# A two-layer hybrid decoder trunk: the preamble's VectorE and ScalarE work in another order, the keys' norm table and the input's quarter sums moved behind it

## The chip, the cores and the metric

One core of a Trainium2 chip. The time is that of one execution of the kernel on the device, in microseconds (us). The profile is of one such execution, recorded by the hardware profiler; it gives every instruction of the five engines: TensorE (PE in the rows, its weight loads PEld), VectorE (DVE), ScalarE (ACT), GpSimd (POOL) and SyncE (SP), and the DMA transfers.

## The reference

The kernel computes two layers of a decoder trunk for 512 tokens of 2048 features in f32. Each layer is an RMS norm, one wide input projection, three mixers that read slices of it, and an output projection into the residual stream:

```python
h = _rmsnorm(x, norm_g)
proj = h @ w_in                    # 2048 -> conv h,b,c,g  512 each; attention q,k,v,g  1024 each;
                                   #         GLA q,k  256 each; GLA v,g  512 each; GLA low rank  16
y_conv = _short_conv(cv_h, cv_b, cv_c, conv_w, conv_b) * silu(cv_g)
q, k = _rmsnorm(sb_q, sb_qn_g), _rmsnorm(sb_k, sb_kn_g)      # per head of 128
y_sb  = _stick_breaking(q, k, sb_v) * silu(sb_g)
g = log_sigmoid(gl_lr @ gla_w_up + gla_b_up) / 16            # GLA: the decay, from the low-rank part
o = _gla(gl_q, gl_k, gl_v, g)                                # chunked linear attention
y_gla = _rmsnorm(o, gla_on_g) * silu(gl_g)
x = x + concatenate([y_conv, y_sb, y_gla]) @ w_out
```

## The kernel before, in words

The tokens are cut into four tiles of 128 (`NT`), the features into 16 blocks of 128 (`KT`), the columns of each weight matrix into pieces of 256 (`GW`). A list, `specs`, names the pieces in the order of their use: GLA's v in two pieces (the second with the 16 low-rank columns), GLA's q, GLA's k, GLA's gate in two pieces, and then those of the convolution, the attention and the output. Each piece is fetched from memory in f32 into one of two staging buffers (`st`).

A matmul in f32 is done as three matmuls in f16: each operand is split into a high and a low part, and high by high, high by low and low by high are summed in PSUM. For a weight piece this means: a maximum over its squares on ACT (`wmax`, L383), a power of two made of it on DVE (`wscale`, L402 to L417), the high part `wh` on ACT (`whi`, L454; L445 and L447 for the very first piece) and the low part `wl` on DVE (`wlo`, L461).

From the GLA gate on, the pieces in the set `quick` are multiplied in Strassen's way (`project_quick`, L794 and L797): seven products of halved matrices instead of eight. That needs sums of quarters of the weights (L527, L529, L532 on DVE), whose high and low parts are L507 on ACT and L508 on DVE, seven of each per piece, and sums of quarters of the input, `xsums` (L734: 20 adds on DVE of 128x1024 in each layer, and eight copies on ACT). In the gate each product is 24 matmuls; the first reads the input itself, the second already the sums.

The input x is prepared in the preamble. Token tile by token tile, and in two halves of 1024 features: the sum of squares on ACT (`xsquare`, L629), the norm's factor on DVE (`xnorm`, L207 to L575), the product with factor and gain on DVE (`xgain`, L580), the transposition by PE into PSUM (`xhigh`, L590) with the copy of the high part out of it by ACT (L592), and the low part (`xlow`): PSUM minus the high part on DVE (L599), or, for the first token tile, with a matmul on PE (L602) and a copy by ACT (L603).

The order of the preamble on DVE and ACT is written out by hand: the calls between `xsquare(0)` and `byhand.__exit__` stand there in the order in which these two engines get them. Everything else is ordered by a scheduler. Each engine works through its own queue in order and waits where an operand or a buffer isn't ready.

The calls behind the preamble are those of layer 0. GLA's v is multiplied (L856), its results are split (`split_v`, L947 and L948). `layer_consts` makes the parameter columns `par` (L294, L295) and the constants of the layers, among them the table `kg` for the keys' norm: a maximum across partitions on POOL, a power of two (L189 to L191), a diagonal matrix (L309), a matmul with ones (L310) and a copy (L311), once per layer. The second piece of v gives the low-rank part too, which is split into bf16 parts and transposed (L980) into the PSUM buffer `tp` and copied to `lrT` (L984). From it, for each of the two halves of GLA's keys, a matmul `gp` (L988) gives the decay: four operations on ACT (L991 to L995), an add on DVE (L996) and four scans on DVE (L999). GLA's k and q are scaled (L1036) and multiplied with the exponentials of the differences of these sums (L1093, L1094, L1102, L1065).

PSUM: the pool `psm` has one buffer, tag "m", which `par`, the `kg` matmuls, `tp` and both `gp` take one after the other.

Of the kernel before, what the change touches and what calls it, by code (L numbers as in the profile page):

```python
# [10 lines left out]
AF = mybir.ActivationFunctionType  # L11
# [32 lines left out]
def hybrid_trunk(ctx, tc, x, norm_g, w_in, conv_w, conv_b, sb_qn_g, sb_kn_g,  # L44
# [8 lines left out]
    GW = 256  # L53
# [238 lines left out]
    def layer_consts():  # L292
        pps = bank(psm, "m")
        T.transpose(pps[:, :NP], prow, ident[:NP, :NP])  # L294
        V.tensor_copy(par, pps[:, :NP])  # L295
        for l in range(depth):
            V.tensor_reduce(onmax[:, l:l + 1], pcol("on", l), AX.X, ALU.max, apply_absolute_value=True)
            V.tensor_scalar(onmax[:, l:l + 1], onmax[:, l:l + 1], float(P) ** 0.5, None, ALU.mult)

            gq = sm(2, "cm")  # L300
            V.scalar_tensor_tensor(gq[:, 0:1], pcol("qn", l), float(P) ** -0.5, pcol("kn", l), ALU.mult, ALU.mult)
            V.tensor_scalar(gq[:, 1:2], allmax(gq[:, 0:1], 1, "k"), 2.0 ** -20, None, ALU.max)
            pow2(zun[:, l:l + 1], gq[:, 1:2], -20.0, "k")
            V.tensor_scalar(nzun[:, l:l + 1], zun[:, l:l + 1], -1.0, None, ALU.mult)
            V.reciprocal(gq[:, 1:2], zun[:, l:l + 1])

            dg = wk([P, P], "e")
            V.tensor_scalar(gq[:, 0:1], gq[:, 0:1], gq[:, 1:2], 2.0 ** -21, ALU.mult, ALU.mult)
            V.tensor_scalar(dg, ident, gq[:, 0:1], None, ALU.mult)  # L309
            T.matmul(pps[:, (l + 1) * P:(l + 2) * P], ones.to_broadcast([P, P]), dg, start=True, stop=True)  # L310
            V.tensor_copy(kg[:, l, :], pps[:, (l + 1) * P:(l + 2) * P])  # L311
            V.tensor_scalar(nbu[:, l, :], par[:, base["bu"] + 2 * l:base["bu"] + 2 * l + 2], -1.0, None, ALU.mult)

# [31 lines left out]

    staged, whole, narrow, peak, scales = {}, {}, {}, {}, {}

# [111 lines left out]
    def wlo(i, h):  # L459
        wh, wl = loaded[i][0][h]  # L460
        V.scalar_tensor_tensor(wl[:, :, :GW], staged[i][h], scales[i], wh[:, :, :GW], ALU.mult, ALU.subtract)  # L461
        if i in narrow:
# [118 lines left out]

    xps = {}

    def xhigh(t, h, dst):

        xv = xt[t // 2][:, t % 2, :]
        xps[t, h] = ps = bank2().rearrange("p a (k c) -> p (a k) c", c=P)
        for i in range(HK):
            k = h * HK + i
            T.matmul(ps[:, i, :], xv[:, k * P:(k + 1) * P], ident, start=i % 4 == 0, stop=True, is_transpose=True,  # L590
                     skip_group_check=True)
        S.activation(dst[0][:, t, h * HK:(h + 1) * HK, :], ps, AF.Copy)  # L592

# [47 lines left out]
    xhigh(0, 0, mix)  # L641
    xsquare(1)
    wscale(0)
    whi0(0, 0, S)
    whi0(0, 1, V)
    xhigh(0, 1, mix)
    whi0(1, 0, V)
# [6 lines left out]
    wlo(0, 0)  # L654
    wlo(0, 1)
    xhigh(1, 0, mix)
    xhigh(1, 1, mix)
    xsquare(2)
    xlow(1, 0, mix, False)
    xlow(1, 1, mix, False)  # L660
    xnorm(0, 2)
    xgain(2, 0)
    xgain(2, 1)
    xsquare(3)
    xnorm(0, 3)
    xhigh(2, 0, mix)
    xhigh(2, 1, mix)
    wmax(1, 0)
    xgain(3, 0)
    xgain(3, 1)  # L670
    xlow(2, 0, mix, False)
    xlow(2, 1, mix, False)
    wmax(1, 1)
    wscale(1)
    xhigh(3, 0, mix)
    xhigh(3, 1, mix)
    whi(1, 0)
    xlow(3, 0, mix, False)
    xlow(3, 1, mix, False)
    wlo(1, 0)  # L680
    whi(1, 1)
# [3 lines left out]
    for l in range(depth):  # L685
# [265 lines left out]
        for t, o, u in project_by_token(xh, xl, GW):  # L951
            begun = split_v(gv[0], t, o[:, :GW])
        if l == 0:
            layer_consts()
# [28 lines left out]
        lrT = wk([P, seq], "e", dt=BF16)  # L983
        V.tensor_copy(lrT, tp)  # L984
        Pc = wk([P, 2, seq], "raw", 1)
        for p in range(2):
# [30 lines left out]
        for tag in ("qT", "kT"):  # L1017
# [23 lines left out]
            if tag == "qT":  # L1041
                insums = xsums()
        gq, gk = qk
        att_u = sm(1, "attu")
# [491 lines left out]
```

## Time and profile before

| | |
|---|---|
| time, median of 3 runs | 1635.48 us (1634.32 to 1636.06) |
| profiled execution: time / span of its instructions | 1638.14 / 1636.3 us |
| PE busy | 1615.8 us (99%) |
| DVE busy | 1445.4 us (88%) |
| ACT busy | 1197.3 us (73%) |
| POOL busy | 274.1 us (17%) |

How to read the rows in the prediction. A row of the timeline has the start in us, the duration, the engine, the line of the kernel, the operation, what it writes, an arrow, what it reads, the shape, and the number of instructions that were put together (x8). What stands in brackets is how long the engine was idle before, and what ended that. A row of the waits has what waited, what it waited for, and then the sum of the waits in us, their number and the longest. A table of stretches has one row for each stretch of the span, with the busy time of each engine in it. Matmuls are pipelined, so the durations of neighbours on PE overlap by more than half; the starts tell the pace.

### The profile page before, as it was taken

To read this page: it belongs to the slowest core of one execution; us is meant where nothing else is said; L and a number is where in the kernel's file an instruction comes from. 1 tells how busy PE (TensorE), PEld (TensorE's weight loads), DVE (VectorE), ACT (ScalarE), POOL (GpSimd) and SP (SyncE) were. 2 spreads that over 40 slices of the span, in tenths; PEclk is the share of its full clock that TensorE was granted. 3 is DMA by queue.
4 is the path that set the end of the run, shared out by engine and by line. 5 is a ranking of instruction groups with operands and counts; after the bars stand their busy time and mean duration, and the time that the engine had idled before them with its cause. 6 is when DMAs were issued, how large, how long until landed. Compare 5 with 4: busy or idle time off the path is not lost.

```text
span 1636.3 us, 42257 instructions
## 1 busy us (share of the span) xinstructions
PE 1615.8 (99%) x18202; PEld 1356.5 (83%) x18202; DVE 1445.4 (88%) x2417; ACT 1197.3 (73%) x1771; POOL 274.1 (17%) x306
## 2 busy tenths in 40 slices
PE   8999999999999999999999999999999999999998
PEld 5758668989999968799996668689898989668998
DVE  7989989989898979898699799898998889898896
ACT  7668886877777777756775787788786868676573
POOL 0122021111212122011102111212121111220110
PEclk9999999999999999999999999999999999999999
DMA  7154435476867686644733544545777876773441
GB/s 262 54 129 134 100 117 105 111 163 147 169 150 168 150 168 193 178 149 142 245 89 105 129 117 109 142 87 138 151 159 158 153 164 150 160 230 129 155 156 54
DMA packets 193644, 235.99 MB, mean 144 GB/s; under 512 B 90242, under 2 KB 153036, under 8 KB 192944
## 3 DMA queue, kind: packets, MB, share of 16 engines
q0 software_dynamic: 79904, 181.42, 41.8%
q1 hardware_dynamic: 104544, 42.42, 13.4%
q10 hardware_dynamic: 9008, 9.45, 1.7%
q8 instruction: 142, 2.33, 0.6%
q14 instruction: 46, 0.38, 0.1%
HBM read 179.65 MB, written 14.68 MB: 119 GB/s over the span
## 4 chain that ended last, share of the span: by engine, by line
PE 69%; DVE 17%; ACT 7%; DMA 4%; issue 3%; POOL 0%; SPq 0%; DVEq 0%; ACTq 0%; POOLq 0%
PE psp L797 23%; PE psp L794 17%; PE psp L712 4%; PE psp L713 4%; PE psp L714 4%; PE psp L703 3%; PE psp L702 3%; PE psp L701 3%; DVE wl L508 3%; PE psp L856 2%; DMA st<-in_w_in_dram 2%; DVE wl L461 2%; PE psm L1342 2%; PE psz L1302 1%; DVE zw L734 1%
## 5 line engine op out<-in xcount | busy, mean ns | idle before, releaser
L507 ACT ACTIVATE wh<-st,ws 128x1024 f16<-128x1024 f32 x270 | 300.6, 1144 | 177.0 <-DVE st L527 89.6
L508 DVE SCALAR_TENSOR_TENSOR wl<-st,ws,wh 128x1024 f16<-128x1024 f32 x270 | 340.2, 1282 | 28.8 <-ACT wh L507 28.6
L383 ACT ACTIVATE junk<-st 128x2048 uint8<-128x2048 f32 x150 | 285.4, 1903 | 13.4 <-DMA st<-in_w_in_dram 7.7
L794 PE MATMUL psp<-s,wh 128*128 128x256 f16 x1280 | 217.7, 273 | 0.1
L794 PEld LDWEIGHTS <-wh 128*128 128x128 f16 x1920 | 187.4, 98 | 23.3 <-issue 1.4
L797 PE MATMUL psp<-wh,s 128*128 128x128 f16 x2048 | 177.2, 219 | 1.7 <-issue 1.6
L794 PE MATMUL psp<-s,wl 128*128 128x256 f16 x640 | 174.3, 273 | 0.9 <-DVE wl L508 0.9
L797 PEld LDWEIGHTS <-s 128*128 128x128 f16 x3072 | 172.9, 98 | 2.1 <-issue 1.8
L712 PE MATMUL psp<-wh,m 128*128 128x256 f16 x640 | 174.5, 273 | 0.0
L714 PE MATMUL psp<-wh,m 128*128 128x256 f16 x640 | 174.5, 273 | 0.0
L713 PE MATMUL psp<-wl,m 128*128 128x256 f16 x640 | 174.5, 273 | 0.0
L797 PE MATMUL psp<-wl,s 128*128 128x128 f16 x1024 | 173.3, 219 | 0.0
L461 DVE SCALAR_TENSOR_TENSOR wl<-st,ws,wh 128x2048 f16<-128x2048 f32 x62 | 145.0, 2349 | 16.1 <-ACT wh L454 15.4
L362 POOL DMA_DIRECT2D st<-in_w_in_dram x114 | 111.1, 1054 | 252.4 <-DVE w7l L508 118.0
L797 PEld LDWEIGHTS <-m 128*128 128x128 f16 x2448 | 139.1, 98 | 2.1 <-issue 1.6
L454 ACT ACTIVATE wh<-st,ws 128x2048 f16<-128x2048 f32 x60 | 118.6, 1999 | 20.9 <-DVE ws L415 11.8
L399 POOL PARTITION_ALL_REDUCE wgm<-wm x75 | 53.5, 713 | 458.7 <-ACT junk L383 443.8
L386 POOL DMA_DIRECT2D st<-st x36 | 57.4, 1593 | 359.3 <-ACT junk L383 340.0
L794 PEld LDWEIGHTS <-wl 128*128 128x128 f16 x960 | 93.9, 98 | 13.5 <-DVE wl L508 1.5
L797 PE MATMUL psp<-wh,m 128*128 128x128 f16 x1088 | 97.2, 219 | 0.4 <-DVE ws L415 0.4
L797 PE MATMUL psp<-wl,m 128*128 128x128 f16 x544 | 93.0, 219 | 0.0
L703 PEld LDWEIGHTS <-wl 128*128 128x128 f16 x384 | 37.6, 98 | 47.7 <-DVE wl L461 3.1
(448 smaller groups left out, 4192.1 us busy)
## 6 DMA issues: line engine op xcount, KB each, us to landing
st<-in_w_in_dram POOLq DMA_DIRECT2D x114, 1024.0 KB, 8.4
st<-in_w_out_dram POOLq DMA_DIRECT2D x32, 1024.0 KB, 8.3
st<-st POOLq DMA_DIRECT2D x36, 512.0 KB, 6.6
st<-in_w_in_dram SPq DMA_DIRECT2D x6, 1024.0 KB, 11.8
mixd<-g POOLq DMA_DIRECT2D x20, 256.0 KB, 7.7
x<-in_x_dram SPq DMA_DIRECT2D x4, 1024.0 KB, 4.8
qT<-in_x_dram ACTq DMA_DIRECT2D x8, 512.0 KB, 4.2
qT<-xs ACTq DMA_DIRECT2D x8, 512.0 KB, 12.3
```

What stands on the lines that cost most here:

```text
L362: load = queue.dma_start(s_, src[l, h * HK * P:(h + 1) * HK * P, c0:c0 + GW].rearrange("(k p) n -> p k n", p=P), max_dma_last_dim=1024)
L383: sq = S.activation(junk(HK * GW).rearrange("p (k n) -> p k n", k=part.shape[1]), part, AF.Square, accum_out=peak[i][:, h:h + 1])
L454: hi = S.activation(wh[:, :, :GW], staged[i][h], AF.Copy, scale=scales[i])
L461: V.scalar_tensor_tensor(wl[:, :, :GW], staged[i][h], scales[i], wh[:, :, :GW], ALU.mult, ALU.subtract)
L507: hi = S.activation(h_, b, AF.Copy, scale=sc)
L508: V.scalar_tensor_tensor(l_, b, sc, h_, ALU.mult, ALU.subtract)
L703: mm = T.matmul(o, wl[:, kk, cs], xh[:, :, k, :], start=False, stop=en)
L712: T.matmul(o, ah[:, t, k, :], wh[:, kk, :n], start=st_, stop=False, skip_group_check=True)
L713: T.matmul(o, ah[:, t, k, :], wl[:, kk, :n], start=False, stop=False, skip_group_check=True)
L714: return T.matmul(o, al[:, t, k, :], wh[:, kk, :n], start=False, stop=en, skip_group_check=True)
L794: mm = T.matmul(o, w[q_][:, kk, :], a[p_][:, :, kk, :], start=st_, stop=en, skip_group_check=True)
L797: mm = T.matmul(o[:, t * P:(t + 1) * P], a[p_][:, t, kk, :], w[q_][:, kk, :], start=st_, stop=en, skip_group_check=True)
```

## The change

`layer_consts` keeps the columns and the small constants; the table `kg` becomes a function of its own, `key_gains`, called once in layer 0 behind `lrT`. The high part of the second half of the first token tile is copied out of PSUM by DVE, not ACT, and the first half piece of the first weights (`whi0(0, 0)`) is made by DVE, not ACT. The hand-written order of the preamble is another one. The quarter sums are held behind low parts of weights (`lows`): in both layers the second half of the steps behind the low part of the piece that was last prepared, in layer 0 the first half behind the low part of v's second piece. The first `split_v` of layer 0 is held behind the copy of the third token tile's first half (`marks`).

```diff
@@ layer_consts
+            V.tensor_scalar(nbu[:, l, :], par[:, base["bu"] + 2 * l:base["bu"] + 2 * l + 2], -1.0, None, ALU.mult)
+
+    def key_gains():
+        pps = bank(psm, "m")
+        for l in range(depth):
             gq = sm(2, "cm")
...
             T.matmul(pps[:, (l + 1) * P:(l + 2) * P], ones.to_broadcast([P, P]), dg, start=True, stop=True)
             V.tensor_copy(kg[:, l, :], pps[:, (l + 1) * P:(l + 2) * P])
-            V.tensor_scalar(nbu[:, l, :], par[:, base["bu"] + 2 * l:base["bu"] + 2 * l + 2], -1.0, None, ALU.mult)
@@ wlo
+        a = V.scalar_tensor_tensor(wl[:, :, :GW], staged[i][h], scales[i], wh[:, :, :GW], ALU.mult, ALU.subtract)
+        lows.setdefault(i, a)
@@ xhigh
-    def xhigh(t, h, dst):
+    def xhigh(t, h, dst, eng=None):
...
-        S.activation(dst[0][:, t, h * HK:(h + 1) * HK, :], ps, AF.Copy)
+        if eng is V:
+            V.tensor_copy(dst[0][:, t, h * HK:(h + 1) * HK, :], ps)
+        else:
+            marks[t, h] = S.activation(dst[0][:, t, h * HK:(h + 1) * HK, :], ps, AF.Copy)
@@ the preamble, by hand
     xsquare(1)
+    xhigh(0, 1, mix, V)
     wscale(0)
-    whi0(0, 0, S)
+    whi0(0, 0, V)
     whi0(0, 1, V)
-    xhigh(0, 1, mix)
     whi0(1, 0, V)
...
     wlo(0, 0)
-    wlo(0, 1)
     xhigh(1, 0, mix)
     xhigh(1, 1, mix)
+    xlow(1, 0, mix, False)
     xsquare(2)
-    xlow(1, 0, mix, False)
-    xlow(1, 1, mix, False)
+    wlo(0, 1)
     xnorm(0, 2)
     xgain(2, 0)
+    xsquare(3)
+    xlow(1, 1, mix, False)
     xgain(2, 1)
-    xsquare(3)
     xnorm(0, 3)
+    wmax(1, 0)
     xhigh(2, 0, mix)
+    xlow(2, 0, mix, False)
+    xgain(3, 0)
+    wmax(1, 1)
     xhigh(2, 1, mix)
-    wmax(1, 0)
-    xgain(3, 0)
+    xlow(2, 1, mix, False)
+    wscale(1)
     xgain(3, 1)
-    xlow(2, 0, mix, False)
-    xlow(2, 1, mix, False)
-    wmax(1, 1)
-    wscale(1)
     xhigh(3, 0, mix)
-    xhigh(3, 1, mix)
     whi(1, 0)
     xlow(3, 0, mix, False)
+    xhigh(3, 1, mix)
+    wlo(1, 0)
     xlow(3, 1, mix, False)
-    wlo(1, 0)
@@ layer 0 and 1, GLA
             begun = split_v(gv[0], t, o[:, :GW])
+            if not l and not t:
+                order(begun, marks[2, 0])
...
         V.tensor_copy(lrT, tp)
+        if l == 0:
+            key_gains()
...
                 insums = xsums()
+                for a in steps[len(steps) // 2:]:
+                    order(a, lows[cursor[0] - 1])
+                if not l:
+                    for a in steps[:len(steps) // 2]:
+                        order(a, lows[1])
```

The lines after the change are some 3 to 16 higher than before: L310 is L314, L461 is L464, L508 is L512, L988 is L999, L996 is L1007, L999 is L1010, L1093 is L1109.

What this makes of the queues is shown at three places. The first is the start of DVE's queue, from the peak of the first weights (L433, L436 after) to the norm's factor of the second token tile (L207). `wh` is the high part of the first weight piece, `wq`, `ws` and `wu` are its scale. Before:

```order
L433 TENSOR_REDUCE wm_29_208<-st_167 128x1
L410 TENSOR_SCALAR wq_227<-psm_228 128x1
L411 TENSOR_SCALAR wq_227<-wq_227 128x1
L415 TENSOR_SCALAR ws_234<-wq_227 128x1
L417 TENSOR_SCALAR wu_236<-wq_227,inoff_156 128x1
L447 TENSOR_SCALAR wh_238<-st_167,ws_234 128x4x256
L447 TENSOR_SCALAR wh_252<-st_167,ws_234 128x4x256
```

And after:

```order
L436 TENSOR_REDUCE wm_29_208<-st_167 128x1
L597 CAST x_185<-psz_227 128x1024
L413 TENSOR_SCALAR wq_237<-psm_238 128x1
L414 TENSOR_SCALAR wq_237<-wq_237 128x1
L418 TENSOR_SCALAR ws_244<-wq_237 128x1
L420 TENSOR_SCALAR wu_246<-wq_237,inoff_156 128x1
L450 TENSOR_SCALAR wh_248<-st_167,ws_244 128x4x256 x2
L450 TENSOR_SCALAR wh_252<-st_167,ws_244 128x4x256
```

A copy of x out of PSUM (L597) has come in ahead of the scale, and both quarters of the first half of the weights are made here, where only one was. On PE, the two matmul pairs that make the first token tile's low parts (L602) now both stand ahead of the first projection matmul; the second pair stood eight matmuls behind it.

The second place is PE's queue just ahead of the GLA gate, whose first matmul is the last row of each piece; L701 to L703 (L708 to L710 after) are the matmuls of GLA's k. Before, the rows around the second `gp`, which stands 70 matmuls ahead of the gate (the first stands 96 ahead):

```order
L703 LDWEIGHTS wl_1040
L703 MATMUL psp_1177<-x_185,wl_1040 128x512
L988 LDWEIGHTS kT_662
L988 MATMUL psm_956<-e_940,kT_662 128x512
L701 LDWEIGHTS wh_1039
L701 MATMUL psp_1177<-x_185,wh_1039 128x512
...
L794 MATMUL psp_1343<-x_185,wh_1218 128x256
```

After:

```order
L999 LDWEIGHTS kT_630
L999 MATMUL psm_957<-e_908,kT_630 128x512
L709 LDWEIGHTS wh_1040
L709 MATMUL psp_1179<-x_186,wh_1040 128x512
L710 LDWEIGHTS wl_1041
L710 MATMUL psp_1179<-x_185,wl_1041 128x512
L801 LDWEIGHTS wh_1219
L801 MATMUL psp_1344<-x_185,wh_1219 128x256
```

The second `gp` has moved to three matmuls ahead of the gate, and the first to 29 ahead. The matmuls of `key_gains` (L314) stand before it, some 83 and 51 matmuls ahead of the gate, where L310 stood in v's projection.

The third place is DVE's queue around the gate's first piece: `wl` and `w7l` are the low parts of its seven weight matrices, from the second on, `st` the quarter sums of the weights, `ga`, `raw` and `e` the decay. Before:

```order
L996 TENSOR_TENSOR ga_958<-ga_958,za_962 128x512
L1065 TENSOR_TENSOR th_988<-e_1820,th_988 128x256
L1065 TENSOR_TENSOR th_988<-e_1856,th_988 128x256
L999 SCALAR_TENSOR_TENSOR raw_942<-ones,ga_958 128x128 x4
...
L508 SCALAR_TENSOR_TENSOR wl_1221<-st_992,ws_1214,wh_1220 128x1024
L527 TENSOR_TENSOR st_992<-st_992 128x8x128
L529 TENSOR_TENSOR st_992<-st_992 128x8x128
L508 SCALAR_TENSOR_TENSOR wl_1219<-st_992,ws_1214,wh_1218 128x1024
L508 SCALAR_TENSOR_TENSOR wl_1221<-st_992,ws_1214,wh_1220 128x1024
L508 SCALAR_TENSOR_TENSOR wl_1223<-st_992,ws_1214,wh_1222 128x1024 x2
L1027 TENSOR_REDUCE gamx_1315<-kT_1173 128x1
L532 TENSOR_TENSOR st_992<-st_992 128x8x128
```

After:

```order
L512 SCALAR_TENSOR_TENSOR wl_1222<-st_993,ws_1215,wh_1221 128x1024
L531 TENSOR_TENSOR st_993<-st_993 128x8x128
L533 TENSOR_TENSOR st_993<-st_993 128x8x128
L1007 TENSOR_TENSOR ga_946<-ga_946,za_950 128x512
L1010 SCALAR_TENSOR_TENSOR raw_943<-ones,ga_946 128x128 x4
L1109 TENSOR_TENSOR e_1821<-raw_943 128x256
...
L512 SCALAR_TENSOR_TENSOR wl_1220<-st_993,ws_1215,wh_1219 128x1024
L512 SCALAR_TENSOR_TENSOR wl_1224<-st_993,ws_1215,wh_1223 128x1024 x2
L405 TENSOR_TENSOR wq_1400<-wgm_1401 128x1
L536 TENSOR_TENSOR st_993<-st_993 128x8x128
L1038 TENSOR_REDUCE gamx_1316<-kT_1174 128x1
L512 SCALAR_TENSOR_TENSOR wl_1222<-st_993,ws_1215,wh_1221 128x1024
```

The first half of the decay (L996, L999, L1093, L1094 before) has come between the sums of the weights and the third low part, the second half of it (with L1102 and L1065) behind the fourth, and the fourth low part (the last row) has changed places with the fifth and sixth.

More of the change, by code (lines that the diff above doesn't have):

```diff
@@ L344, in hybrid_trunk @@
     cursor = [0]
-    staged, whole, narrow, peak, scales = {}, {}, {}, {}, {}
+    staged, whole, narrow, peak, scales, lows = {}, {}, {}, {}, {}, {}
     def junk(n):
@@ L460, in wlo @@
         wh, wl = loaded[i][0][h]
-        V.scalar_tensor_tensor(wl[:, :, :GW], staged[i][h], scales[i], wh[:, :, :GW], ALU.mult, ALU.subtract)
+        a = V.scalar_tensor_tensor(wl[:, :, :GW], staged[i][h], scales[i], wh[:, :, :GW], ALU.mult, ALU.subtract)
+        lows.setdefault(i, a)
         if i in narrow:
@@ L580, in xgain @@
         V.scalar_tensor_tensor(xv, xv, xscale[t], gb[h], ALU.mult, ALU.mult)
-    xps = {}
-    def xhigh(t, h, dst):
+    xps, marks = {}, {}
+    def xhigh(t, h, dst, eng=None):
         xv = xt[t // 2][:, t % 2, :]
```

## The prediction

> **What bounds the kernel now.** I read the busy times first, then what TensorE (PE) waits for, then a table of stretches, and last the timelines of the places that the change touches. From the page:
>
> ```profile
> PE 1615.8 (99%) x18202; PEld 1356.5 (83%) x18202; DVE 1445.4 (88%) x2417; ACT 1197.3 (73%) x1771; POOL 274.1 (17%) x306
> ```
>
> PE is busy in 1615.8 of 1636.3 us, so an edit that leaves its matmuls as they are, as this one does, can gain 20.5 us at the very most. The waits of PE, first in the span's first 110 us, then from 110 to 1300 us:
>
> ```profile
> PE psp L856 <- ACT wh L445: 1.5, 1, 1.5
> PE psp L703 <- DVE wl L461: 1.3, 1, 1.3
> PE psz L590 <- DVE x L580: 1.2, 1, 1.2
> PE psz L590 <- DVE x L599: 1.2, 1, 1.2
> PE psp L856 <- ACT wh L456: 0.6, 1, 0.6
> PE psp L856 <- DVE kpc L190: 0.6, 1, 0.6
> PE psp L856 <- ACT x L592: 0.2, 1, 0.2
> ...
> PE psp L794 <- DVE wl L508: 0.9, 2, 0.5
> PE psp L703 <- DVE wl L461: 0.8, 1, 0.8
> ```
>
> The first seven rows are the preamble. The L580 wait (1.2) comes before the first matmul on x and no edit touches what it waits for. The other six sum to 5.4 us, and that is the stake. Afterwards PE hardly waits: the two last rows are 1.7 us in 1190. What could spend the gain again is VectorE (DVE). The table of stretches gives start:end, length, then busy us of PE, PEld, DVE, ACT and POOL:
>
> ```profile
> 20.00:76.00 56.00, 51.98 (x434) 43.48 (x433) 54.87 (x103) 39.91 (x51) 5.24 (x6) 1.00 0.37 111
> ...
> 100.00:118.00 18.00, 18.00 (x87) 8.27 (x86) 13.10 (x34) 12.27 (x18) 2.71 (x3) 1.00 0.47 129
> 118.00:140.00 22.00, 22.00 (x225) 19.41 (x223) 20.99 (x37) 16.20 (x23) 3.13 (x4) 1.00 0.52 121
> 140.00:160.00 20.00, 20.00 (x223) 15.90 (x221) 19.00 (x38) 19.44 (x32) 4.17 (x6) 1.00 0.36 110
> 160.00:180.00 20.00, 20.00 (x167) 9.20 (x165) 19.34 (x49) 16.05 (x33) 1.84 (x2) 1.00 0.52 129
> 180.00:200.00 20.00, 19.54 (x206) 17.06 (x205) 19.59 (x33) 16.95 (x24) 3.81 (x4) 1.00 0.49 105
> ```
>
> DVE is full from 20 to 76 us (54.87 of 56), has 4.9 us free between 100 and 118, and is full again from 118 to 200 (78.92 of 82, 3.08 idle). A PE that arrives earlier at 118 us meets a DVE that has nothing to give, unless DVE comes earlier too. That is the whole question of this change.
>
> **The change part by part.** I count PE's lead, the time by which it is earlier than before at the same matmul.
>
> *The start.* PE's timeline, and the split of the first weights on DVE and ACT:
>
> ```profile
> 10.84 3.68 PE L590 MATMUL psz<-ident,x 128*128 128x128 f32 x16 [1.20 <-DVE x L580]
> ...
> 18.00 1.87 PE L856 MATMUL psp<-wh,x 128*128 128x256 f16 x8 [1.54 <-ACT wh L445]
> 19.66 1.06 PE L602 MATMUL psz<-x,ga 128*128 128x512 f16 x2
> 20.52 3.50 PE L856 MATMUL psp<-wh,x 128*128 128x256 f16 x16
> 23.86 1.04 PE L590 MATMUL psz<-ident,x 128*128 128x128 f32 x8
> 24.73 1.04 PE L856 MATMUL psp<-wh,x 128*128 128x256 f16 x8
> 25.60 1.04 PE L590 MATMUL psz<-ident,x 128*128 128x128 f32 x8
> ...
> 16.20 1.41 DVE L447 TENSOR_SCALAR wh<-st,ws 128x1024 f16<-128x1024 f32 x2
> 27.01 2.35 DVE L599 TENSOR_TENSOR x<-psz,x 128x1024 f16<-128x1024 f32 x2
> ...
> 16.82 1.13 ACT L445 ACTIVATE wh<-st,ws 128x1024 f16<-128x1024 f32 x1
> ```
>
> The first projection matmul waits 1.54 us for a piece that ACT writes until 17.95. Now DVE writes it, behind a copy of the second half of x out of PSUM. That copy is not in the trace. The nearest row is L599, which reads the same 128x1024 from PSUM and a second operand, 2.35 for two; ACT's piece of that size took 1.13. I take 1.2, with nothing below 1.1 and nothing above half of 2.35 and a bit, 1.25. The transposes that it needs are over at 10.84 + 3.68 = 14.5, so it ends near 15.7, about when DVE starts its scale work for the row of 16.20: it lies in idle time of DVE. The two halves (1.41) then end near 17.7. Meanwhile PE does the second pair of L602 (1.06), which stood at 19.66. So the wait shrinks from 1.54 to about 0.3: gain 1.2.
>
> *The other preamble waits.* The reordering puts the residues of x (L599) and the last weight splits ahead of squares, gains and quarter sums, and the kg work, whose wait (kpc L190, 0.6) goes with its matmuls. Four waits, 1.3, 1.2, 0.6 and 0.6, can go whole: 3.7. The one of 0.2 stays. New ones can open, since PE now arrives earlier at what DMA and ACT give: nil at least, and at most what the three small waits of today are, 0.6 + 0.6 + 0.2 = 1.4. I take 1.1, near the upper end, since DVE's total work before 76 us is not made much smaller and it had only 1.13 us idle in 56. Lead at the start of the GLA gate's first matmul: 1.2 + 3.7 - 1.1 = **3.8 us**, bounds 3.5 and 4.9.
>
> *kg moved behind lrT.* Its small DVE rows are the same ones at another time. But it takes the only buffer of psm, in which the decay's two matmuls gp (L988, L999 after) must then wait. And the order now puts the first gp 29 matmuls ahead of the gate where 96 stood before, the second 3 ahead where 70 stood.
>
> ```profile
> 96.91 0.38 PE L988 MATMUL psm<-e,kT 128*128 128x512 bf16 x1
> ...
> 102.52 0.38 PE L988 MATMUL psm<-e,kT 128*128 128x512 bf16 x1
> ...
> 117.41 0.38 PE L703 MATMUL psp<-x,wl 128*128 128x512 f16 x1
> 117.63 0.27 PE L794 MATMUL psp<-x,wh 128*128 128x256 f16 x1
> ...
> 125.60 0.27 PE L794 MATMUL psp<-s,wl 128*128 128x256 f16 x1
> ```
>
> With 117.63 - 117.41 = 0.22 us from matmul to matmul, the gate starts at 117.63 - 3.8 = 113.8, the first gp comes at 113.8 - 29 x 0.22 = 107.4 instead of 96.91, the second near 113.1 instead of 102.52. No matmul waits for that by itself: but DVE's work on the decay leaves the slack between 100 and 118 and falls among the gate's weight splits. DVE there, before:
>
> ```profile
> 102.49 0.42 DVE L1093 TENSOR_TENSOR e<-raw 128x256 f32<-128x256 f32 x1
> ...
> 106.77 0.76 DVE L1102 SCALAR_TENSOR_TENSOR e<-e,qT 128x256 f32<-128x256 f32 x2 [1.40 <-ACT qT L1036]
> 107.87 0.69 DVE L996 TENSOR_TENSOR ga<-ga,za 128x512 f32<-128x512 f32 x1 [0.33 <-ACT ga L993]
> 108.48 0.75 DVE L1065 TENSOR_TENSOR th<-e,th 128x256 f16<-128x256 f32 x2
> 109.15 1.36 DVE L999 TENSOR_TENSOR_SCAN raw<-ones,ga 128x128 f32<-128x128 f32 x4
> ...
> 113.61 1.28 DVE L508 SCALAR_TENSOR_TENSOR wl<-st,ws,wh 128x1024 f16<-128x1024 f32 x1 [2.25 <-ACT wh L507]
> ...
> 118.58 4.88 DVE L508 SCALAR_TENSOR_TENSOR wl<-st,ws,wh 128x1024 f16<-128x1024 f32 x4 [1.17 <-ACT wh L507]
> 123.37 0.68 DVE L1027 TENSOR_REDUCE gamx<-kT 128x1 f32<-128x512 f32 x1
> 123.97 1.22 DVE L532 TENSOR_TENSOR st<-st 128x1024 f32<-128x1024 f32 x1
> ```
>
> After the change the order on DVE is: second split; two sums; the first half of the decay (one add, four scans, four differences); third split; fifth and sixth; L532's sum; L1027's reduction; only then the fourth. Times: the second split still follows PE (its ACT half waits for a buffer that PE frees), so 113.61 - 3.8 = 109.8. The split (1.28) and two sums of L532's kind (1.22 each) end at 113.6. The decay is 0.69 + 1.36 + 4 x 0.42 = 3.7, less about 0.3 as neighbours overlap: 117.0. Three splits at 4.88 / 4: 120.7. Sum, reduction and fourth split, 1.22 + 0.68 + 1.28 less 0.2 of overlap: 123.7. PE wants the fourth split's low part 125.60 - 117.63 = 7.97 us into the gate, at 121.8. It waits **1.9 us** (before, the fourth stood second in the row of 118.58, done by 118.58 + 2 x 1.22 = 121.0, with 4.6 to spare). Lead left: 1.9.
>
> *Behind the gate.* At 123.7 DVE has done what it had done at 125.1 before (L532 over), less what it still owes: L1102, L996, L1065 and the second scans, 0.76 + 0.69 + 0.75 + 1.36 = 3.56. So it stands where it stood at 121.5: 2.2 us late, while PE is 1.9 early. From there to 200 us DVE had 3.08 us of idle time to catch up with, and at 189.86 PE already waited for a split (the 0.46 that PE lacks in the row 180 to 200). PE's lead at 190 us thus lies between -2.2 (no idle time recovered) and +1.9 (all that is needed). Neither end is nearer to a row, so I take the middle, **-0.15**.
>
> *The quarter sums held behind the low parts.* Twenty adds, the same ones; in layer 0 they end before the gate in both orders. In layer 1 the low part comes sooner, which can end the 0.8 wait of L703 for wl, and the sums come later for the next reader: between +0.8 and -0.8; I take nothing. The rest (a tile's split behind a mark, nbu earlier) is 0.15 us rows of DVE and goes for nothing.
>
> *Clock.* From 20.52 to the next start at 23.86, 16 matmuls take 3.34 us; from 24.73 to 25.60, 8 take 0.87: 0.21 us and 0.11 each, so half pace until about 23.8 and full pace after it. PE is now nearly gapless from 15 instead of 18. If full pace came one such stretch earlier, the 16 matmuls would take 16 x 0.109 = 1.74 instead of 3.34: 1.6 us. I put nothing into the sum, since the lead is cut back to DVE's time in the gate anyway. The Trainium skill (TensorE: Matmul & The Clock Gate, Part 1: The HAM clock gate) says that the clock goes from half to full after one busy window of about 3.4 us, whose start is not tied to the kernel; by that an estimate would be 1.7 us less, if the window before is filled now.
>
> *Sum.* The profiled execution took 1638.14 us (span 1636.3 and 1.84 around it); lead -0.15 gives 1638.3. The median of the runs shown is 1635.48, so there 1635.6.
>
> **The rivals.**
> *A, the lead is kept.* If DVE recovers, or the fourth split comes in time, 3.8 stays, and with the 0.8 of layer 1 it is 4.6: 1630.9. For it: six real waits go, and DVE had 3.08 us idle after 118. Against it: DVE 96% busy (78.92 of 82) where it would have to catch up.
> *B, earlier full pace.* The 1.6 of the rows of 20.52 to 25.60, on top of the middle: 1634.0; only with the 1.9 of lead left kept at 190 as well it gives 1635.48 - 1.9 - 1.6 = 1632.0. For it: PE's gapless start. Against it: where DVE is full, an earlier PE only waits longer. It is also what the Trainium skill's page on the clock gate (TensorE: Matmul & The Clock Gate, Part 1) would lead one to expect.
> *C, slower.* The single psm buffer: the decay comes 10.5 us later (107.4 for 96.91), and all of GLA hangs on it through a DVE without slack. If DVE's lateness at 123.7 is doubled, as the second gp is as late, 2 x 2.2 = 4.4 us are lost: 1639.9. It decides from the point at which PE's lead at 200 us is under -3.3. For it: a full DVE. Against it: only 0.9 us of PE waits there today, and 3.08 us idle.
> *D, the change does not do what it says.* New waits take the place of the old ones in the preamble (lead 1 or less), and with DVE's 2.2: up to 1637.7, within the same bound.
>
> **How the numbers follow.** About 0.2%, 3.3 us, is what a measurement can tell from no change: faster is below 1632.2, slower above 1638.8. Forecast (-2.2 to +1.9, with 0.8 either way: 1632.8 to 1638.5) 0.46; A 0.23; B 0.10, of which 0.04 goes under 1632.2; C 0.16; D 0.05. Faster 0.23 + 0.04 = 0.27; slower 0.16; same 0.57. The range reaches from 1631.0, into A, to 1639.3, into C, leaving out about 0.1 on either side.
>
> **What would show it.** PE's waits for L445's, L599's, kpc's and L461's successors gone before 76 us, and the first matmul that reads x as tokens for GLA's queries some 4 us earlier; the gate's first matmul near 113.8; a PE wait of about 2 us some 8 us into the gate, for DVE's wl; gp near 107 and 113. Wrong it would be if PE passes the gate without a wait (then A), if waits for DVE between 125 and 207 sum to over 4 us (C), or if the gate starts later than 116 (D).

## The result and the profile after

The changed kernel takes 1639.74 us (median of 8, 1637.77 to 1641.80) where the kernel before takes 1635.93 (median of 8): 1.0023 of the time, 95% interval 1.0014 to 1.0032. It is slower by 3.8 us, just above the upper end of the range that was predicted (1639.3). The profiled execution took 1638.41 us with a span of 1636.4, the third shortest of its eight; that of before, 1638.14, is longer than all eight of its own (1634.32 to 1637.48). So the two profiles differ by 0.3 us where the medians differ by 3.8, and the place of the loss has to be read from the waits, not from the two spans.

What PE waits for in the changed kernel, up to 130 us (without the first row, which lies ahead of the preparation of x) and from there to the end (sum in us, times, longest):

```profile
PE psz L594 <- DVE x L584: 2.9, 2, 1.6
PE psp L801 <- DVE wq L414: 2.3, 1, 2.3
PE psm L294 <- DMA e<-in_gla_on_g_dram: 1.3, 1, 1.3
PE psp L863 <- DVE wh L450: 0.6, 1, 0.6
PE psp L863 <- ACT x L599: 0.4, 2, 0.2
...
PE psz L1185 <- DVE e L1173: 2.0, 1, 2.0
PE psz L1137 <- DVE zw L1123: 1.0, 1, 1.0
```

The waits of the preamble that the prediction counted are gone (for kpc, L456, L461 and L599 by the old numbers) or small (L450, 0.6 instead of 1.5); two new ones, 1.3 for parameter rows that DMA has not landed and 1.3 for the gain of x (the second of the two waits for L584), stand in their place. Two new ones of some 2 us are behind the preamble: 2.3 in the GLA gate and 2.0 before the GLA products (L1185, the matmuls with GLA's v). PE's timeline at the gate, and the first of the GLA products:

```profile
106.85 0.38 PE L999 MATMUL psm<-e,kT 128*128 128x512 bf16 x1
...
112.46 0.38 PE L999 MATMUL psm<-e,kT 128*128 128x512 bf16 x1
...
113.11 0.27 PE L801 MATMUL psp<-x,wh 128*128 128x256 f16 x1
...
123.51 0.28 PE L801 MATMUL psp<-s,wl 128*128 128x256 f16 x1 [2.27 <-DVE wq L414]
...
124.50 0.27 PE L801 MATMUL psp<-s,wl 128*128 128x256 f16 x1
...
125.54 0.42 PE L801 MATMUL psp<-s,wl 128*128 128x256 f16 x1
...
194.99 0.83 PE L1185 MATMUL psz<-th,v 128*128 128x128 f16 x12 [1.97 <-DVE e L1173]
```

And DVE's in the same stretch:

```profile
113.31 0.69 DVE L1007 TENSOR_TENSOR ga<-ga,za 128x512 f32<-128x512 f32 x1
114.03 1.37 DVE L1010 TENSOR_TENSOR_SCAN raw<-ones,ga 128x128 f32<-128x128 f32 x4
...
116.79 3.67 DVE L512 SCALAR_TENSOR_TENSOR wl<-st,ws,wh 128x1024 f16<-128x1024 f32 x3
120.37 0.15 DVE L405 TENSOR_TENSOR wq<-wgm 128x1 f32<-128x1 f32 x1
120.44 1.22 DVE L536 TENSOR_TENSOR st<-st 128x1024 f32<-128x1024 f32 x1
121.58 0.68 DVE L1038 TENSOR_REDUCE gamx<-kT 128x1 f32<-128x512 f32 x1
122.17 1.28 DVE L512 SCALAR_TENSOR_TENSOR wl<-st,ws,wh 128x1024 f16<-128x1024 f32 x1
```

The gate starts at 113.11 instead of 117.63, so PE is 4.5 us early; it stands from 121.24 to 123.51 for the fourth low part, which DVE ends at 122.17 + 1.28 = 123.45, behind the decay (L1007, L1010). The profile names wq (L414) as the releaser, a row that ends together with it; the low part is what PE reads. One more thing shows in the durations: the same matmul takes 0.27 us at 124.50 and 0.42 at 125.54. The table of stretches of this kernel (start:end, length, busy time of PE, PEld, DVE, ACT and POOL, then the granted clock, the DMA share and GB/s) says why:

```profile
117.00:121.00 4.00, 4.00 (x39) 3.55 (x37) 4.00 (x5) 4.00 (x6) 0.00 (x0) 1.00 0.41 47
121.00:125.00 4.00, 1.73 (x16) 1.31 (x14) 4.00 (x9) 3.31 (x7) 1.29 (x1) 0.97 0.00 0
125.00:129.00 4.00, 4.00 (x24) 3.00 (x23) 4.00 (x12) 2.57 (x3) 1.81 (x2) 0.61 0.20 19
129.00:133.00 4.00, 4.00 (x39) 3.58 (x37) 4.00 (x10) 0.00 (x0) 0.00 (x0) 1.00 0.92 327
```

Behind the wait the granted clock is halved for 3.4 us (0.61 as the mean of 4 us: 24 matmuls where 39 go in the next row). So the wait is paid nearly twice: 2.3 and another 1.7. DVE has 4.00 of 4.00 in all four rows.

The ledger of PE's lead over the kernel before, at the same matmul in both profiles: +4.5 us at 121 us, +0.4 at 133, -2.6 at 206. The waits between are 2.27, 0.54, 0.96, 0.32 and 1.97 (6.06 in sum) against 0.46 before, and half a clock for 3.4 us is 1.7: 7.3, and the ledger fell by 7.1. In layer 1 the wait of L703 is gone, which gives about +1, and at 1280 us the ledger stands at -2.0. Then it jumps to -0.2, for a wait that, of the two, only the kernel before has; its profile names no releaser for it ("issue"):

```profile
1292.05 0.29 PE L797 MATMUL psp<-wh,s 128*128 128x128 f16 x2 [1.64 <-issue]
```

That is how the two profiles come to end only 0.3 us apart.

### The profile page after: what moved, and what is told of

Its sections match the earlier page's. It is cut to its first block, busy times and chain, and to the rows that moved or that the text cites. A ratio compares the mean times of both kernels' runs of the same rounds, so it can differ in the third digit from the quotient of the medians.

```text
span 1636.4 us, 42255 instructions
## 1 busy us (share of the span) xinstructions
PE 1614.2 (99%) x18202; PEld 1355.8 (83%) x18202; DVE 1447.2 (88%) x2419; ACT 1194.7 (73%) x1769; POOL 273.1 (17%) x306
## 4 chain that ended last, share of the span: by engine, by line
PE 70%; DVE 14%; ACT 6%; DMA 5%; issue 2%; SPq 2%; POOL 0%; DVEq 0%; ACTq 0%; POOLq 0%
PE psp L804 23%; PE psp L801 14%; PE psp L863 6%; PE psp L719 4%; PE psp L720 4%; PE psp L721 4%; DVE wl L512 3%; PE psp L709 3%; PE psp L708 3%; PE psp L710 3%; DMA st<-in_w_in_dram 2%; DMA th<-za 2%; PE psm L1358 1%; ACT wh L511 1%; ACT junk L386 1%
## 5 line engine op out<-in xcount | busy, mean ns | idle before, releaser
L512 DVE SCALAR_TENSOR_TENSOR wl<-st,ws,wh 128x1024 f16<-128x1024 f32 x270 | 340.3, 1282 | 30.1 <-ACT wh L511 30.0
L386 ACT ACTIVATE junk<-st 128x2048 uint8<-128x2048 f32 x150 | 285.3, 1902 | 15.5 <-DMA st<-in_w_in_dram 9.0
L464 DVE SCALAR_TENSOR_TENSOR wl<-st,ws,wh 128x2048 f16<-128x2048 f32 x62 | 145.3, 2349 | 13.4 <-ACT wh L457 12.3
L710 PEld LDWEIGHTS <-wl 128*128 128x128 f16 x384 | 37.6, 98 | 44.2
```

The lines of the kernel that those rows point to most:

```text
L386: sq = S.activation(junk(HK * GW).rearrange("p (k n) -> p k n", k=part.shape[1]), part, AF.Square, accum_out=peak[i][:, h:h + 1])
L464: a = V.scalar_tensor_tensor(wl[:, :, :GW], staged[i][h], scales[i], wh[:, :, :GW], ALU.mult, ALU.subtract)
L512: V.scalar_tensor_tensor(l_, b, sc, h_, ALU.mult, ALU.subtract)
```

## The experiments

Theory: the key table, made behind `lrT`, takes the one buffer of `psm` and pushes the decay's matmuls into the gate, so that its work falls among the weight splits of a full DVE; PE waits, and the clock falls. Rivals: DVE's load itself, wherever the table stands; the new preamble; chance of the clock. Medians with the ratio to the kernel before on the same chip (its own median there is 1635.44 or 1635.72):

| run | what it is | median us | ratio (95%) |
|---|---|---|---|
| again | the changed kernel | 1639.15 | 1.0023 (1.0014 to 1.0032) |
| kg_back | key table back in its old place | 1632.69 | 0.9981 (0.9973 to 0.9990) |
| kg_late | key table behind decay and masks | 1636.06 | 1.0001 (0.9992 to 1.0010) |
| kg_only | before, key table moved | 1637.78 | 1.0018 (1.0010 to 1.0027) |
| kg_psz | changed, key table in another buffer | 1632.62 | 0.9985 (0.9976 to 0.9994) |
| lows_only | before, holds only | 1632.30 | 0.9979 (0.9970 to 0.9988) |
| lows_kg | before, holds, key table moved | 1638.62 | 1.0016 (1.0007 to 1.0024) |
| pre_only | new preamble only | 1640.89 | 1.0034 (1.0021 to 1.0048) |
| fill | changed, PE kept busy in the gate's wait | 1638.65 | 1.0015 (1.0006 to 1.0023) |
| par_late | kg_back, parameter columns later | 1631.01 | 0.9972 (0.9960 to 0.9983) |
| par_kg_late | par_late, table's matmuls to be held: no instruction moved | 1631.50 | 0.9977 (0.9968 to 0.9986) |
| lows_start | holds and the new start | 1630.03 | 0.9970 (0.9958 to 0.9981) |

**again**, the changed kernel unaltered.

> The changed kernel once more, unaltered. Theory (a PE wait of 2.3 us in the GLA gate's first piece, and a stretch of 3.4 us at half clock directly behind it, 1.7 us lost, sometimes with a further such stretch behind the 1 to 2 us waits near 180 and 195 us): the same wait and stretch in this profile, time 1637.5 to 1642, and the executions with the lower mean clock are the longer ones, by about 1.7 us for each 0.001 of it. Rival (the half clock strikes by chance and has nothing to do with the wait): a profile with no half-paced stretch near 124 us, or one elsewhere, and as often in the kernel before; time near 1636.

The waits are the same (2.27 in the gate at 125 us, 1.97 at 195), the half clock is not: in this execution it follows the two waits near 30 us and the one at 195, and not the one in the gate.

```profile
28.00:32.00 4.00, 1.92 (x14) 1.55 (x15) 2.94 (x13) 3.32 (x6) 1.36 (x1) 0.96 0.63 191
32.00:36.00 4.00, 4.00 (x25) 3.17 (x24) 4.00 (x13) 3.05 (x4) 0.00 (x0) 0.61 1.04 338
191.00:195.00 4.00, 2.03 (x24) 1.50 (x19) 4.00 (x12) 2.88 (x7) 1.84 (x2) 1.00 0.24 44
195.00:199.00 4.00, 4.00 (x32) 3.21 (x31) 3.97 (x5) 1.71 (x3) 0.00 (x0) 0.57 1.02 363
```

Each halved stretch comes right behind 4 us in which PE was busy for half (1.92, 2.03). Which of the waits is hit changes from one execution to the next. The expectation that length and mean clock go together held only loosely: 1636.6 at 1.000, 1637.5 to 1640.1 at 0.999, 1638.2 to 1641.4 at 0.998, 1640.5 at 0.997.

**kg_back** and **kg_late**, the key table elsewhere in the changed kernel:

```diff
             layer_consts()
+            key_gains()              # kg_back
...
         V.tensor_copy(lrT, tp)
-        if l == 0:
-            key_gains()
...
             make_masks()
+            key_gains()              # kg_late
```

> The changed kernel, but the key table is made right behind the parameter columns again, as before; the rest of the change stays. Theory (the key table's place in the single psm buffer pushes the decay's matmuls into the gate): gp is back at over 50 matmuls ahead of the gate, no PE wait over 0.5 us in the gate, no half clock, PE's lead of 4.5 us at the gate kept past 130 us, and 1631 to 1634. Rival (DVE is full, so any lead is taken back wherever the key table stands): waits of 2 us or more in the gate or near 180 to 200 us all the same, 1635 to 1640.

> The changed kernel, but the key table is made behind the decay and the masks, not ahead of the decay. Theory (what costs is the order in the psm buffer, not that the key table's work lies late): gp again over 50 matmuls ahead of the gate, waits in the gate under 1 us, 1631 to 1635. Rival (the key table's work on DVE costs wherever it lies behind the preamble): as the changed kernel, 1637 to 1641.

kg_back: 1632.69, as the theory had it; no wait of PE over 0.7 us behind 60 us, and PE's lead at 75 us stays almost whole to the end of layer 0 (1.5). It is only 1.8 us, not 4.5 (1.7 lie in a halved stretch at 31 us, and a 1.3 wait for v's split at 48 is new). So the move of the table, on top of the rest, costs 6.5 us. kg_late fell between: gp is early again and the gate has no wait, but at 184 us PE waits 0.6, and then the GLA products wait, by more than in the changed kernel (the clock is halved there for 6.8 us, from 190 to 197):

```profile
PE psz L1184 <- DVE e L1172: 2.8, 1, 2.8
PE psp L801 <- DVE wl L512: 0.6, 1, 0.6
```

Its decay is not late at all. DVE's scans stand at

```profile
99.05 1.36 DVE L1008 TENSOR_TENSOR_SCAN raw<-ones,ga 128x128 f32<-128x128 f32 x4
106.54 1.37 DVE L1008 TENSOR_TENSOR_SCAN raw<-ones,ga 128x128 f32<-128x128 f32 x4
```

where the kernel before has them at 100.91 to 102.46 and from 109.15. So the wait before the GLA products can come without a late decay; what makes it in kg_late is not shown.

**kg_psz**, one name altered in the changed kernel:

```diff
     def key_gains():
-        pps = bank(psm, "m")
+        pps = bank2()[:, 0, :]
```

> The changed kernel with one name altered: the key table's matmuls take a buffer of psz, not the only one of psm; their place behind lrT and DVE's work for them stay. Theory (the single psm buffer is what pushes gp into the gate): gp 84 and 58 matmuls ahead of the gate, no wait over 0.5 us in the gate; what may stay is a wait of up to 2.7 us of the GLA products near 190 us, as in kg_late, since DVE still does the table's rows in its slack; 1632 to 1636.5. Rival (DVE's work for the table behind lrT is the cost, the buffer is not): the gate waits 2 us as in the changed kernel, 1637.5 to 1641.

Theory, and better than it had it: 1632.62. In PE's timeline both gp (L999) stand far ahead of the gate again, by 87 and 60 matmuls (96 and 70 in the kernel before, 29 and 3 in the changed one), each ahead of the table's matmuls (L314), and the gate starts as early as in the changed kernel:

```profile
94.69 0.38 PE L999 MATMUL psm<-e,kT 128*128 128x512 bf16 x1
94.91 0.38 PE L314 MATMUL psz<-e,ones 128*128 128x128 f32 x2
100.31 0.38 PE L999 MATMUL psm<-e,kT 128*128 128x512 bf16 x1
102.47 0.38 PE L314 MATMUL psz<-e,ones 128*128 128x128 f32 x2
113.05 0.27 PE L801 MATMUL psp<-x,wh 128*128 128x256 f16 x1
```

The fourth low part now ends at 121.6, and PE waits 0.5 for it instead of 2.3. PE's lead over the changed kernel grows from 0 at 100 us to 1.9 in the gate and 6.4 at 204. The table's work on DVE lies behind `lrT` here too, and the GLA products do not wait; so it was the buffer. (This profile has a halved stretch of its own, at 1288 us, behind a wait of 2.4 us on "issue"; its execution, 1635.12, is the longest of its eleven.)

**kg_only** and **lows_kg**, the table moved as the change does, with the preamble as before, without and with the holds.

> The kernel before with one edit of the change alone: the key table behind lrT, ahead of the decay. Preamble, quarter sums and marks are as before. Theory: the same wait of about 2 us in the gate although PE has hardly any lead (the split that it waits for follows PE's own pace), half clock behind it when the wait falls so; 1636.5 to 1641. Rival (the loss comes from the lead meeting a full DVE, not from the key table): no wait over 0.5 us in the gate, 1634.5 to 1636.5.

> The kernel before with the holds of the quarter sums and the key table behind lrT; the preamble is as before. Theory (the table's place costs by itself, whatever PE's lead): a wait of 1 to 2.3 us in the gate, waits of GLA behind it; 3 to 7 us over lows_only (1632.3): 1635.5 to 1639. Rival (it costs only where the new preamble has made PE early): no wait over 0.5 us in the gate, 1631.5 to 1633.5.

kg_only: 2.3 us over before, within the theory's range, but with a smaller wait: 1.2 and 0.6 in the gate's first piece and 1.3 in its second, and no half clock. lows_kg against lows_only: 6.3 us more (6.1 by the ratios, as the two ran on different chips). The size came out, the place did not: no wait in the gate's first piece at all, but

```profile
PE psz L1180 <- DVE e L1168: 2.8, 1, 2.8
...
PE psp L798 <- ACT wh L511: 0.9, 1, 0.9
PE psp L798 <- DVE wl L512: 0.9, 1, 0.9
```

and a halved clock for 3.4 us behind the first of them. So the table's place costs with the old preamble too, and costs more where PE has a lead to lose. By the ledger, kg_only goes from 0.9 ahead of the kernel before at 121 us to 2.9 behind it at 210, lows_kg from 4.3 ahead to 1.9 behind, the changed kernel from 4.5 ahead to 2.6 behind; kg_psz goes from 4.6 to 3.8 ahead. Where the loss falls differs: in kg_only, as in `fill` below, the decay is as late as in the changed kernel and the GLA products do not wait; in lows_kg they do. Which order on DVE makes that wait stays open.

**lows_only**, the holds alone in the kernel before:

```diff
                 insums = xsums()
+                for a in steps[len(steps) // 2:]:
+                    order(a, lows[cursor[0] - 1])
+                if not l:
+                    for a in steps[:len(steps) // 2]:
+                        order(a, lows[1])
```

> The kernel before with the holds of the quarter sums alone. Theory: the two waits of L703 for wl (1.3 and 0.8) go, nothing else moves: 1633.3 to 1634.6. Rival (the sums come late for the gate's second product, or push DVE's later work): new waits for DVE at 118 to 125 us or past 180 us, 1635 to 1638.

3.4 us gained, over a microsecond more than the two waits that were to go. The waits for wl (1.3), for L456 (0.6) and for kpc (0.6) at 47 to 76 us are all gone, and L703's in layer 1 as well; what is left up to 230 us, besides those ahead of the first matmul on x and two of 0.2:

```profile
PE psz L591 <- DVE x L600: 1.2, 1, 1.2
PE psp L857 <- ACT wh L445: 1.2, 1, 1.2
PE psp L795 <- DVE wl L509: 0.4, 1, 0.4
```

The sums' adds, 1.22 each, had stood between small rows that PE's next weights hang on, here those that make the scale of v's second piece (DVE's timeline of the kernel before, and then the same row `ws` in lows_only, 3.6 us earlier):

```profile
41.99 1.22 DVE L734 TENSOR_TENSOR zw<-x,g 128x1024 f32<-128x1024 f16 x1
43.12 0.15 DVE L402 TENSOR_TENSOR wq<-wgm 128x1 f32<-128x1 f32 x1
...
43.26 1.22 DVE L734 TENSOR_TENSOR zw<-zw,x 128x1024 f32<-128x1024 f32 x1
44.39 0.15 DVE L411 TENSOR_SCALAR wq<-wq 128x1 int32<-128x1 int32 x1
...
44.51 1.22 DVE L734 TENSOR_TENSOR zw<-x,zw 128x1024 f32<-128x1024 f16 x1
45.65 0.15 DVE L415 TENSOR_SCALAR ws<-wq 128x1 int32<-128x1 int32 x1
```

```profile
42.02 0.14 DVE L415 TENSOR_SCALAR ws<-wq 128x1 int32<-128x1 int32 x1
```

**pre_only**, kg_back without the holds and the mark.

> kg_back without the holds: neither the quarter sums behind the low parts nor the first split behind the mark; what is left of the change is the hand-written order, the copy and the first high part on DVE. Theory (the holds take away the waits of L703 for wl, 1.3 at 76 us and 0.8 in layer 1, and no more): 1 to 2.2 us over kg_back, 1633.5 to 1635. Rival 1 (the hand-written order alone carries it): as kg_back, 1632 to 1633.3. Rival 2 (it carries nothing): as the kernel before, 1635 to 1636.

All three expectations were wrong: 5.2 us slower than before. What the scheduler puts first on DVE behind the new hand-written order are the sums: three of them (L741) from 38.99 to 43.06, among and ahead of the rows that make the scale of v's second piece (wq, ws). ACT's high part of it comes late:

```profile
PE psz L594 <- DVE x L584: 4.2, 4, 1.6
PE psp L863 <- ACT wh L459: 4.0, 2, 3.3
```

The 3.3 are followed by 3.4 us at half clock at 54 us. The new order needs the holds: with both and the table in its old place 1632.69, with neither 1635.4, with the order alone 1640.89. The holds don't need the order: alone they give 1632.30.

**fill**, 20 matmuls of a tile of zeros in the changed kernel, where PE waits in the gate; they add zero to the sum.

```diff
+                            if kk == 0 and i == 1:
+                                for _ in range(fill):
+                                    T.matmul(o, scr[0][:, 1, 1, :P], a[0][:, :, kk, :], start=False, stop=False,
+                                             skip_group_check=True)
...
-            prod(pd, wT3, a11_21, end is not None)
+            prod(pd, wT3, a11_21, end is not None, fill=20 * (cols and not l and cursor[0] == 5))
```

> The changed kernel with 20 matmuls more, of a tile of zeros, added into the gate's fourth product ahead of its first low part, where PE waits 2.3 us: they add nothing to the sum, and at 0.11 us each they fill 2.2 us. DVE's order around the gate is that of the changed kernel; some rows behind it change places. Theory (it is PE's idle time that brings the half clock): the next matmul starts as late as in the changed kernel, but no half clock follows the gate; the time is at most 1.7 us less, 1637 to 1639. Rival 1 (half clock comes from something else in the gate, or by chance): it still follows the gate in some executions, time as the changed kernel, 1638.5 to 1640. Rival 2 (PE's time counts and DVE's does not): the 20 matmuls are added to the time, 1640.5 or more.

PE's timeline at the gate, with the 20 matmuls in one row, and then the stretches:

```profile
121.05 2.35 PE L802 MATMUL psp<-s,qp 128*128 128x256 f16 x20
123.49 0.28 PE L805 MATMUL psp<-s,wl 128*128 128x256 f16 x1
```

```profile
121.00:125.00 4.00, 3.91 (x36) 3.27 (x35) 4.00 (x9) 3.28 (x7) 1.29 (x1) 1.00 0.00 0
125.00:129.00 4.00, 4.00 (x39) 3.59 (x38) 4.00 (x12) 2.46 (x3) 1.81 (x2) 1.00 0.18 16
```

The low part is as late as ever (the next matmul at 123.49, in the changed kernel 123.51), but the clock stays at 1.00 and 39 matmuls go where 24 went. Over its eleven executions the mean clock lacks 0.0006 of full speed, in `again` 0.0016, a difference of 1.6 us in 1638. The median is only 0.5 lower than that of `again`, and its executions spread from 1634.1 to 1641.1, four of the five longest at a mean clock of 1.000; DVE's rows behind the gate have changed places too (the wait of 1.97 before the GLA products is not there, for one), so the time doesn't measure the clock's share. What makes its long executions long stays open.

**par_late**, **par_kg_late** and **lows_start**, towards a faster version. The first holds the transposition of the parameter rows in kg_back behind a copy of ACT, the second was to hold the table's matmuls in par_late as well; the third is lows_only with the copy and the first weight piece on DVE.

```diff
-        T.transpose(pps[:, :NP], prow, ident[:NP, :NP])
+        order(T.transpose(pps[:, :NP], prow, ident[:NP, :NP]), marks[2, 0])     # par_late
...
+            order(T.matmul(pps[:, (l + 1) * P:(l + 2) * P], ...), lows[1])       # par_kg_late
...
     xsquare(1)
+    xhigh(0, 1, mix, V)                                                          # lows_start
     wscale(0)
-    whi0(0, 0, S)
+    whi0(0, 0, V)
     whi0(0, 1, V)
-    xhigh(0, 1, mix)
```

> kg_back with one more edit: the transposition of the parameter rows (L294) is held behind ACT's copy of the third token tile's first half, so that PE and DVE no longer stand before rows that DMA has not landed (PE 1.7 us, DVE 1.67 us in kg_back, at 27 to 29 us). Theory (two waits within one stretch of 3.4 us make the half clock at 31 us): L294 without a wait, no half clock before 100 us, and 1.5 to 3.5 us less than kg_back: 1629 to 1631.5. Rival (DVE is full, the time comes back as another wait before 76 us): as kg_back, 1632 to 1634.

> par_late with the matmuls of the key table held behind the low part of v's second piece, as PE stood 1.1 us before the first of them (L314 at 44.7 us). Theory: that wait goes, no wait over 0.7 us in the gate or behind: 1629 to 1630.7. Rival (DVE is the bound before 76 us, the wait comes back at the next matmul): as par_late, 1630.7 to 1631.5.

> lows_only with the new start: DVE copies the second half of the first token tile and makes the first weight piece; the rest of the preamble as before. Theory (the start's gain of 1.2 us, and of as much again where full pace comes earlier, is kept as nothing is queued in DVE for it): 1629.8 to 1631.5. Rival (PE's earlier start only meets the next wait, L599's at 39 us, which grows): 1632 to 1633.

par_late came as expected (1631.01): no wait for DMA, no half clock in its profile, 1.7 us less than kg_back. par_kg_late is par_late over again (1631.50): the low part behind which the table's matmuls were held had ended at 43.0 us, and PE, DVE, ACT and POOL run the same instructions in the same order in both profiles. The wait is there as it was (at 44.73 in par_late):

```profile
44.65 0.49 PE L314 MATMUL psm<-e,ones 128*128 128x128 f32 x2 [1.13 <-DVE e L313]
```

So neither its theory nor its rival was tested, and the 0.5 us between the two medians is what two runs of the same order, on different chips, can differ by. lows_start has the lowest median, 5.4 us below the kernel before, though the wait for the parameter rows (1.6) is in it; by its ratio it can't be told from par_late (0.9970 and 0.9972). The rest of the hand-written order was not needed for it.

## Why the prediction was wrong

*The lead.* 3.8 was predicted at the gate's start, 4.5 came (bounds 3.5 to 4.9). Of the terms, the start was too small: its wait shrank by 0.9 (1.54 to 0.64, with 1.2 predicted), but full pace came at 15.5 us and not at 23.8, and at 20 us the lead was 3.0 already. The new waits were too small as well (1.3 and 1.3 against 1.1), so that the sum was nearer than its terms.

*The gate.* Right nearly to the digit: gp at 106.85 and 112.46 (107.4 and 113.1 predicted), the fourth low part done at 123.45 (123.7), a wait of 2.27 (1.9). That the single psm buffer makes it is shown by kg_psz.

*Behind the gate.* Here it failed. The step before the sum, "PE's lead at 190 us thus lies between -2.2 ... and +1.9 ... I take the middle, -0.15", came near by luck: of the -2.6 at 206 us, waits of 0.32 at 191 and 1.97 at 195 were still to come at 190, which leaves about -0.3 there (an estimate from these rows). But the way was another one. The prediction had 1.9 behind the gate and 2.05 lost to DVE from there; what came was 0.4 at 133, as the clock took 1.7, and some 0.7 lost. The step that failed is the next one, "lead -0.15 gives 1638.3": it closes the account at 190 us and at full clock. Two terms were put at nothing. The first is the GLA products, whose waits at 191 and 195 took 2.3 us; DVE's idle time, which was to help, stayed idle: 3.07 us from 118 to 200 here, 3.08 before. That the late decay makes these waits is not shown: kg_late has them without it, `fill` and kg_only have it without them. The second is the clock, priced in one direction alone, as a gain at the start ("I put nothing into the sum"). The wait that the prediction itself had found in the gate halves the clock behind it in some executions: 1.7 us a time. The mean clock lacks 0.0019 in the eight executions, 3.1 us of 1638, and 0.0007, 1.1 us, in the runs of before beside `again`: about 2.0 of the 3.8 us, if lost clock is lost time, which `fill` could not show.

*What the two profiles hide.* They end 0.3 us apart where 0.15 was predicted, and that is luck too: the -2.0 of 1280 us is mostly made up by the 1.64 us for which the kernel before waits at 1292. The prediction's two rows from 110 to 1300 us, "1.7 us in 1190", left out four rows of the same view, 3.5 us in sum, with this wait as the largest; so its starting point of 1638.14 was an execution 2.2 us above the median of before (1635.93).

*The rivals.* C, slower by the single psm buffer, was the one that happened, at nearly the predicted price (4.4 lost where 3.8 were). But doubling DVE's lateness was a guess of the size, and in the profiled execution both of its signs were just missed: the lead behind the GLA products was -2.6 where it asked for under -3.3, and the waits for DVE from 125 to 207 us summed to 3.8 where it asked for over 4. It had not counted the clock. The kernels kg_back and kg_psz put the buffer at 6 to 7 us, against some 2.7 that the holds and the rest had earned. B's earlier full pace came, and is in the lead of 4.5. D happened in part: two new waits in the preamble, without the small lead. A (the lead kept) is what kg_psz shows: 1632.62, against 1630.9 predicted for it.

*The holds.* The prediction took them for nothing; alone they are worth 3.4 us. Three of the waits that they end (1.3, 0.6 and 0.6) it had credited to the new order of the preamble. Reading "Twenty adds, the same ones" it overlooked what had stood behind them in DVE's queue.

*The clock.* From row to rule: in the traces' clock records, a stretch between two changes lasts 3.41 us or a whole multiple of it (17.07, 109.23, 160.43), so each execution has a grid of 3.41 us. Counted on that grid, in windows at full clock, PE's idle shares of 0.53 to 0.86 were followed by a halved window eleven times in the thirteen profiles beside that of before (two of these halvings lie in the kernel's last 3 us; windows without any matmul are not counted). Four shares from 0.50 to 0.58 were not. Of the smaller shares only one, 0.28 in kg_late, was followed by a halved window, and that one prolonged a halved stretch. In the changed kernel's profile the gate's wait lies in one window (0.64); in `again` it is split over two (0.26 and 0.40), and no halving follows. The Trainium skill (TensorE: Matmul & The Clock Gate, Why this matters for your kernels) asks for no idle gaps of over about 3 us between matmuls; here gaps of 2 us were enough in several executions, so the measurement decides. That the window does not start anew with the kernel, as the Trainium skill says in Part 1 of that page, agrees with the same wait being hit in one execution and spared in the next.

## What to carry to other kernels

When work is moved, list what it holds as well as what it does: a buffer of which there is one makes everything that needs it next wait, and here that moved two matmuls and the work behind them out of DVE's slack. On a kernel whose PE is 99% busy, price a new PE wait of some 2 us at its length and, in the executions in which the clock is halved behind it, at 1.7 us more; two waits of 1.3 us close together had the same effect in `again`. Carry the sum to the end of what hangs on the moved work, not to the last wait that the profile before shows. And long operations of one engine that nobody needs soon should be held behind the short ones on which the next weights hang: this was the part of the change that paid.

## What the runs showed of the hardware

A wait of PE of about 2 us, well short of the 3.4 us for which the clock then stays halved, can halve it where it falls into one window of the 3.41 us grid: the gate's 2.27 us did so in the changed kernel's profile and not in `again`, the 1.97 us at 195 did so in `again` and not in the first. This is a part of why the changed kernel's times spread over 4.8 us (1636.63 to 1641.44 in `again`), but not all: at one mean clock, 0.998, they run from 1638.16 to 1641.44.
